# Joining the small products of three token mixers into fewer, larger steps between GEMM matmuls

## The chip, the cores and the metric

The kernel runs on one core of a Trainium2 chip. The metric is the device time of one execution in microseconds (us), the median over runs.

## The reference

One layer of a hybrid decoder: 512 tokens behind 16 learned meta tokens, width 1024, all in float32.

```python
h = RMSNorm(z);  P = h @ W_in
y = sigmoid(G_gla)*(GLA(P) W_a) + sigmoid(G_rwkv)*(RWKV7(P) W_b) + sigmoid(G_hgrn)*(HGRN2(P) W_c)
z = z + y @ W_out
z = z + ConvFFN(RMSNorm(z))        # D_FF 2816, then a last RMSNorm
...
# GLA (4 heads) and HGRN2 (4 heads), in chunks
scores = einsum('bhnid,bhnjd->bhnij', q * exp(b - b_ref), k * exp(b_ref - b))      # masked causal
o_intra = einsum('bhnij,bhnjv->bhniv', scores, v)
inc = einsum('bhnjd,bhnjv->bhndv', k * exp(b_last - b), v)
s_next = dec[..., None] * s + inc
o_inter = einsum('bhnid,bhndv->bhniv', q * exp(b), s_start)
...
# RWKV7 (8 heads of 64): S is 64x64 per head
s = s * w_t + sa[..., None] * (kk_t * a_t) + v_t[..., None] * k_t      # sa = -S kk_t
y_t = S r_t
```

## The kernel before, in words

**GEMMs.** The projections are computed transposed, 128 output columns at a time and all 528 (or 512) tokens in two halves. Each float32 weight tile is split on ACT (L202) and DVE (L203) into two float16 parts, and three float16 products are summed for each pair, so PE runs thousands of matmuls of 128x128 weights on 256 to 272 columns ("GEMM matmul" below; out `g`). Three weight buffers w0 to w2 rotate; the GEMM's outputs use two pairs of PSUM banks, g0 and g1.

**Mixers.** GLA, HGRN2 and RWKV7 need many small float32 products: transposes, scores of chunks, state updates, with meta tokens (16 rows) treated apart. Their outputs use a ring of four PSUM banks: each call of `bank` takes the next, and PE waits until the former user of that bank has been copied out by ACT or DVE. `lin_mixer` (L580 on) serves four HGRN2 heads (hg0 to hg3, one head each) and GLA (gl0, gl1, two heads each). Its steps: transposes of k (`pk`, `pmt`), of v (`pv`, one per head), state of the meta tokens and increments (`ps0`, `pin`), scores (`pc`), those of the meta tokens (`pcm`), outputs (`po`), meta outputs (`pom`), transposed outputs (`pt`, `ptm`). `rw_phase1` prepares pairs of RWKV7 heads i=0 to 3 (`psu`, `psa`, norms of k in `pss`, `prb`, `pM`, meta `pMm`). An inversion of triangular blocks runs on DVE (L1194, L1199). `rw_phase2` forms `pQ`, `pN`, transposes `tA`, `tB`, `tK`, `tV`, the meta part `tm` with `pmm`, then `psb`, `psx`, `p1`, `p2`, `pw`, `ph`/`py`, `pf`, and a chain of eight steps `pc` for two heads each, which hands a state on through a copy to HV (L1473, L1474), with a norm (L1440 to L1444) and `pyt` behind it.

**What sets the order.** On PE the order is the program's own. `drive` runs all mixers as generators: a mixer yields (delay, banks wanted) ahead of a step and is resumed when PE's modelled time has passed the delay, so many banks are modelled free, and enough GEMM matmuls have been issued since the last step (0.7 of that step's modelled time, and always one matmul at least). The delays stand in the table LT. What a mixer issues between two yields is called a step here; between two steps lie GEMM matmuls. The order on DVE, ACT and POOL is made by a scheduler from priorities, so it moves when the steps do.

```python
        yield LT["pk"][im], 2
...
            yield LT["pv"], 1
...
                    owed = LT["mix"] * (pe.t - t0) + 0.01
```

Of the kernel before, what the change touches and what calls it, by code (L numbers as in the profile page):

```python
# [48 lines left out]
LT = dict(  # L49
    f=17.0, pk=(1.0, 1.89, 0.0, 0.0, 1.0, 0.0), pv=0.0, ps0=1.2, pc=0.75,  # L50
    po=(4.08, 2.75, 0.98, 0.0, 0.0, 2.0), pt=(10.56, 10.58, 9.41, 18.52, 18.27, 9.18), gk=0.75, v=0.0,
    gv=4.09, k=4.31, pss=(1.14, 1.4, 0.28, 1.69), prb=(2.37, 3.25, 2.02, 2.9),
    pM=(2.7, 3.05, 4.48, 2.95), pMm=0.0, r=18.93, rv=0.9, g=1.82, T=53.8, pN=0.0, tA=2.44, tB=0.0, tK=0.8,
    tm=3.44, psb=1.1, psx=1.06, p1=11.9, p2=3.06, pw=5.19, ph=0.44, pf=0.1, ch0=0.0, ch=3.4, gn=3.11, y=9.68,
    hold=1.85, mix=0.7,
)
# [38 lines left out]
def trunk(ctx: ExitStack, tc: tile.TileContext, d: dict, out: bass.AP):  # L95
# [486 lines left out]
    def lin_mixer(im, gev, nm, gsum, gscale, q, k, vs, sgs, normw, ys):  # L582
# [84 lines left out]
        vec.tensor_copy(S[:, 0], ps0)  # L667
        for t in range(3):
            vec.scalar_tensor_tensor(S[:, t + 1], S[:, t], DT[:, t : t + 1], pin[:, t, :], ALU.mult, ALU.add)


        yield LT["pc"], 2
# [27 lines left out]
        for pcm, hr in zip(pcms, hrs):  # L700
            pe.matmul(pcm, lhsT=k1[hr, 0:16], rhs=q1[hr, 14:16], start=True, stop=True)
        for (st, stm), pcm in zip(stv, pcms):
            vec.copy_predicated(stm, maskC[0:16, 14:16], pcm)
# [526 lines left out]
    def rw_phase2(i, r1, E0, ANs, Xs, HVs, s2, s2m, s3):  # L1230
# [75 lines left out]
        pa = tok4(f"tA{i}", Ap, 0)
        for rr, kc in par:
            act.activation(AN[rr, :, :, rr], pa[rr], AF.Copy)

        for h, hr in enumerate(hrs):  # L1310
            for q, (rr, sr_) in enumerate(par):
# [9 lines left out]
        pk = tok4(f"tK{i}", Kd, 16)
        for q, (rr, sr_) in enumerate(par):
            act.activation(E[sr_, q:8:2, :, sr_], pk[sr_], AF.Copy)
        yield f"v{i}"
        yield 0.0, 1

# [486 lines left out]
```

## Time and profile before

| | |
|---|---|
| runs | 1023.19, 1027.21, 1027.33 us; median 1027.21 |
| profiled execution | 1026.22 us, span 1023.9, granted clock 0.99 |
| busy PE / weight loads (PEld) / DVE / ACT / POOL | 96 / 76 / 62 / 46 / 14% of the span |

The mixers run from about 30 to 580 us, the last GEMMs and the FFN behind them. Records of PE overlap, since a matmul drains while the next streams: distances between starts tell what one costs, not the length of a record. A float32 product is two records on PE. Waits are given as "engine waits for a tile <- engine and line that released it".

### The profile page before, as it was taken

What the parts mean: (1) busy time and instruction counts of PE and PEld (TensorE: products, weight loads), DVE (VectorE), ACT (ScalarE), POOL (GpSimd) and SP (SyncE); (2) the same over time, 40 slices, a digit from 0 to 9 for tenths busy, and PEclk for the clock granted to TensorE, in tenths of its full rate; (3) what the DMA queues carried; (4) which work ended last, traced back from release to release, by engine and by line L of the source; (5) the groups of instructions that cost most, each with busy time, mean ns of one, the idle gap of its engine ahead of it and who ended that gap; (6) DMA issues with size and microseconds to landing.
All of it is one profiled execution on the core that took longest, in us unless ns stands there. A gap on an engine that the chain in (4) does not pass through costs nothing.

```text
span 1023.9 us, 20898 instructions
## 1 busy us (share of the span) xinstructions
PE 984.7 (96%) x8694; PEld 775.6 (76%) x8694; DVE 638.2 (62%) x1234; ACT 467.1 (46%) x882; POOL 140.4 (14%) x307
## 2 busy tenths in 40 slices
PE   8999989999999989999999989999999999999996
PEld 7888877887778868788878874488888888854442
DVE  5677655445677998677644485567777677783211
ACT  6767565435654444344433353553334443552100
POOL 3122211201333511111000123000000000000100
PEclk9999999999999999999999999999999999999999
DMA  6322222233224314122233463023333333472100
GB/s 192 106 69 58 63 63 83 63 94 81 84 70 115 91 46 126 39 67 63 59 87 84 126 226 106 1 84 104 104 92 96 102 104 104 146 229 99 42 14 28
DMA packets 149289, 92.35 MB, mean 90 GB/s; under 512 B 17664, under 2 KB 142073, under 8 KB 149195
## 3 DMA queue, kind: packets, MB, share of 16 engines
q1 hardware_dynamic: 149195, 91.02, 31.3%
q8 instruction: 68, 1.11, 0.5%
q14 instruction: 26, 0.21, 0.1%
HBM read 86.92 MB, written 3.95 MB: 89 GB/s over the span
## 4 chain that ended last, share of the span: by engine, by line
PE 72%; DVE 12%; ACT 7%; DMA 3%; issue 3%; POOL 2%; SPq 0%; POOLq 0%; DVEq 0%; ACTq 0%
PE g L70 56%; PE dn L70 6%; DVE w L203 2%; DVE AN L1199 1%; DVE HV L1194 1%; DMA wf<-in_w_out_dram 1%; PE pc L70 1%; ACT w L202 1%; PE pf L70 1%; PE hT L75 1%; PE pw L70 1%; PE pogl L70 1%; ACT L383 1%; DMA z<-in_x_dram 1%; PE pcgl L70 0%
## 5 line engine op out<-in xcount | busy, mean ns | idle before, releaser
L70 PEld LDWEIGHTS <-w 128*128 128x128 f16 x5856 | 570.2, 99 | 89.4 <-issue 9.2
L70 PE MATMUL g<-hT,w 128*128 128x256 f16 (+3 forms) x5280 | 620.5, 274 | 2.6 <-ACT siluhg L383 2.2
L203 DVE SCALAR_TENSOR_TENSOR w<-wf,w 128x1024 f16<-128x1024 f32 (+1 forms) x131 | 150.7, 1151 | 93.8 <-ACT w L202 93.5
L202 ACT ACTIVATE w<-wf 128x1024 f16<-128x1024 f32 (+1 forms) x131 | 130.6, 999 | 108.0 <-PE g L70 96.1
L70 PEld LDWEIGHTS <-hid 128*128 128x128 f16 x528 | 51.7, 98 | 63.0 <-issue 1.1
L70 PE MATMUL g<-y,w 128*128 128x258 f16 x576 | 75.3, 273 | 3.5 <-DVE y L447 2.0
L1691 DVE SCALAR_TENSOR_TENSOR c<-u,parB,c 128x512 f32<-128x512 f32 x88 | 66.1, 751 | 2.4
L70 PE MATMUL g<-wd,hid 128*128 128x512 f16 x264 | 57.3, 379 | 0.8 <-DVE z L1742 0.8
L70 PE MATMUL dn<-wd,hid 128*128 128x512 f16 x264 | 57.1, 379 | 0.0
L1746 POOL TENSOR_SCALAR ssf<-ssf 128x1 f32<-128x1 f32 x4 | 2.2, 540 | 311.2 <-ACT sq L1744 311.1
L70 PE MATMUL g<-woh,mT 128*128 128x512 f16 x128 | 38.9, 379 | 0.6 <-DVE z L1645 0.6
L1709 ACT ACTIVATE c<-c 128x512 f32<-128x512 f32 x22 | 13.9, 630 | 53.8 <-DVE c L1691 53.8
L1744 ACT ACTIVATE sq<-z 128x512 f32<-128x512 f32 x8 | 5.0, 628 | 72.3 <-DVE z L1742 72.3
L70 PEld LDWEIGHTS <-mT 128*128 128x128 f16 x192 | 18.5, 98 | 24.2 <-issue 2.9
L1725 DVE SCALAR_TENSOR_TENSOR wd<-wf,wd 128x1024 f16<-128x1024 f32 x22 | 26.9, 1224 | 15.6 <-ACT wd L1724 15.4
L1724 ACT ACTIVATE wd<-wf 128x1024 f16<-128x1024 f32 x22 | 23.3, 1057 | 25.1 <-DMA wf<-in_w_down_dram 25.1
L1443 POOL TENSOR_TENSOR gv<-gv,mhalf 128x2 f32<-128x2 f32 (+1 forms) x16 | 13.9, 876 | 136.2 <-DVE gv L1442 136.2
L1742 DVE SCALAR_TENSOR_TENSOR z<-g,z 128x512 f32<-128x512 f32 x4 | 2.8, 692 | 45.8 <-PE g L70 45.8
L383 ACT ACTIVATE u<-g 128x258 f32<-128x258 f32 x88 | 29.2, 373 | 0.0
L1474 ACT ACTIVATE HV<-pc 64x128 f32<-64x128 f32 x32 | 8.4, 272 | 42.8 <-DVE HV L1473 39.4
L70 PE MATMUL g<-wol,mT 128*128 128x512 f16 x64 | 24.3, 379 | 0.0
L1689 DVE TENSOR_SCALAR c<-u,parB 128x512 f32<-128x512 f32 x44 | 23.8, 542 | 0.0
(484 smaller groups left out, 1195.6 us busy)
## 6 DMA issues: line engine op xcount, KB each, us to landing
wf<-in_w_in_dram SPq DMA_DIRECT2D x65, 512.0 KB
wf<-in_w_up_dram SPq DMA_DIRECT2D x44, 512.0 KB
wf<-in_w_down_dram SPq DMA_DIRECT2D x22, 512.0 KB
wf<-in_w_out_dram SPq DMA_DIRECT2D x8, 512.0 KB
xt<-in_x_dram SPq DMA_DIRECT2D x4, 512.0 KB
wf<-in_w_out_hg_dram SPq DMA_DIRECT2D x8, 256.0 KB
wf<-in_w_out_gla_dram SPq DMA_DIRECT2D x8, 256.0 KB
...
```

Source lines behind the costliest of these rows:

```text
L70: r = self.eng.matmul(out, lhsT=lhsT, rhs=rhs, **kw)
L75: r = self.eng.transpose(out, in_, ident)
L202: act.activation(wh[:, :kt, :m], wf[:, :kt, :m], AF.Copy, scale=WS)
L203: vec.scalar_tensor_tensor(wl[:, :kt, :m], wf[:, :kt, :m], WS, wh[:, :kt, :m], ALU.mult, ALU.subtract)
L383: act.activation(dst[:m, off + c0 : off + c0 + n], src, func, **kw)
L1194: eng.tensor_tensor(u, bc(mats[:, j, j + 1 : n], c1 - c0), Ti[:, j, c0:c1].unsqueeze(1).broadcast_to([cnt, r, c1 - c0]), op=ALU.mult)
L1443: gps.tensor_tensor(var, var, mhalf[:, 0 : 2 * n].rearrange("p (a b) -> p a b", b=2), op=ALU.pow)
L1689: vec.tensor_scalar(c, u[:, 0:SEQ], colB(52 + j), colB(8 + j), ALU.mult, ALU.add)
L1691: vec.scalar_tensor_tensor(c, u[:, t : t + SEQ], colB(52 + 44 * t + j), c, ALU.mult, ALU.add)
L1709: act.activation(cg, cg, AF.Silu)
L1724: act.activation(wd[f][:, 0], wf, AF.Copy, scale=WS)
L1725: vec.scalar_tensor_tensor(wd[f][:, 1], wf, WS, wd[f][:, 0], ALU.mult, ALU.subtract)
```

## The change

Two steps become one where the second had only been put behind a yield; what belongs together also shares banks:

- `lin_mixer`: `pv` of all heads follows `pk` in one step, which asks for 2 banks and one more per head. `pcm` moves from behind `pc` into the step of `ps0`/`pin` and uses free columns of their banks. `pom` moves from behind `po` to behind `pc`, in one bank for all heads, and is copied out after `po`.
- `rw_phase1`: the five products `pss` lose the yields between them. `pMm` joins `pM` in its banks.
- `rw_phase2`: `pmm` moves from the `tm` step to `pN`, in its banks; its six copies to Xm, Em, Nm come before those of `pN`. `tA` and `tB` become one step, `tK`, `tV` and `tm` another (3 banks). `ph`/`py` join `pw` in one bank. The two heads of a chain step follow each other with no yield.
- The delays in LT become one number per mixer, with the same values. Lines shift by 29 to 31.

```diff
-        yield LT["pk"][im], 2
+        yield LT["pk"][im], 2 + nh
...
         for h in range(nh):
-            yield LT["pv"], 1
             pv = bank(f"pv{nm}{h}", P, 4, P)
...
-        yield LT["ps0"], 2
-        ps0 = bank(f"ps0{nm}", P, P)
-        pin = bank(f"pin{nm}", P, 3, P)
+        yield LT["ps0"][im], 2
+        psb0, pinb = bank(f"ps0{nm}", P, 512), bank(f"pin{nm}", P, 512)
+        ps0, pin = psb0[:, 0:P], pinb[:, 0 : 3 * P].rearrange("p (t n) -> p t n", n=P)
+
+        pcms = [psb0[0:16, P : P + 2], pinb[0:16, 3 * P : 3 * P + 2]][:nh]
...
+        for pcm, hr in zip(pcms, hrs):
+            pe.matmul(pcm, lhsT=k1[hr, 0:16], rhs=q1[hr, 14:16], start=True, stop=True)
+        for (st, stm), pcm in zip(stv, pcms):
+            vec.copy_predicated(stm, maskC[0:16, 14:16], pcm)
...
         for (st, stm), pc in zip(stv, pcs):
             vec.copy_predicated(st, maskC.unsqueeze(1).broadcast_to([P, 4, P]), pc)
-        yield 0.0, 2
-        pcms = [bank(f"pcm{nm}{h}", 16, 2) for h in range(nh)]
...
+        poms = bank(f"pom{nm}", 2, nh, P)
+        for h in range(nh):
+            pe.matmul(poms[:, h, :], lhsT=stv[h][1], rhs=mt[:, 1 + h, :], start=True, stop=True)
...
-        yield 0.0, 2
-        poms = [bank(f"pom{nm}{h}", 2, P) for h in range(nh)]
-        for h, pom in enumerate(poms):
-            pe.matmul(pom, lhsT=stv[h][1], rhs=mt[:, 1 + h, :], start=True, stop=True)
...
             pe.matmul(pss[:, t, :], lhsT=kq[:, 16 + P * t : 16 + P * (t + 1)], rhs=ind2, start=True, stop=True)
-            yield 0.0, 0
...
+        for pm, hr in zip(pms, hrs):
+            pe.matmul(pm, lhsT=BKm[hr, 0], rhs=AR[hr, 0, 0:16], start=True, stop=True)
...
-        yield LT["pMm"], 2
-        pms = [bank(f"pMm{i}{h}", 16, 16) for h in range(2)]
...
-        yield LT["tA"], 1
+        yield LT["tA"][i], 2
         pa = tok4(f"tA{i}", Ap, 0)
+        pb = tok4(f"tB{i}", Bd, 16)
...
-        yield LT["tB"], 1
-        pb = tok4(f"tB{i}", Bd, 16)
...
-        yield LT["tK"], 1
+        yield LT["tK"][i], 3
         pk = tok4(f"tK{i}", Kd, 16)
...
-        yield LT["tm"], 2
...
-        pms = [bank(f"pmm{i}{h}", 16, 20) for h in range(2)]
...
-        yield LT["pw"], 2
+        yield LT["pw"][i], 3
...
-        yield LT["ph"], 2
-        ph = bank(f"phm{i}", 64, 2, 64)
-        py = bank(f"pym{i}", 2, 2, 64)
+        phy = bank(f"phm{i}", P, 512)
...
                     pe.matmul(pc[:, l, :], lhsT=E[:, c, l, :], rhs=HV[:, c, l, :], start=True, stop=True)
-                    if l == 0:
-                        yield 0.0, 0
```

PE in HGRN2 head 3 (`hg3`), before: `pcm` and `po` each stand as a step between GEMM matmuls (`g`).

```order
L70 MATMUL g_70<-hT,w_76 128x258
L70 MATMUL pcmhg_1836<-e1hg_1701,d1hg_1702 16x2
L70 LDWEIGHTS w_76
L70 MATMUL g_70<-hT,w_76 128x256
L70 MATMUL pohg_1840<-vthg_1763,st_409 128x128 x4
L70 MATMUL pohg_1840<-Shg_1765,q5hg_1730 128x128 x4
```

The same after the change, the steps of `ps0` and of `pc` (13 GEMM matmuls stand between `pomhg` and `pohg`, left out here).

```order
L101 MATMUL ps0hg_1786<-mthg_1748 128x128
L101 MATMUL pinhg_1787<-vthg_1755,kthg_1743 128x128 x3
L101 MATMUL ps0hg_1786<-e1hg_1698,d1hg_1699 16x2
...
L101 MATMUL pchg_1805<-qmhg_1731,kmhg_1732 64x64 x4
L101 MATMUL pchg_1805<-bhg_1696,dlhg_1706 32x32 x8
L101 MATMUL pomhg_1823<-mthg_1748,stm_410 2x128
```

`pcm` (16x2, out in the bank of `ps0`) and `pom` have moved ahead, behind other small products.

ACT in the first GLA pair (`gl0`), before: `vt` are copies of `pv`, `silu` and `w` belong to the GEMM.

```order
L653 ACTIVATE vtgl00_2169<-pvgl00_2164 128x512
L383 ACT_TABLE_LOAD
L383 ACTIVATE silugl00_2173<-g1_70 128x258
L383 ACTIVATE silugl00_2173<-g1_70 128x256
L202 ACTIVATE w0_74<-wf0_71 128x1024
L653 ACTIVATE vtgl01_2185<-pvgl01_2180 128x512
L594 ACT_TABLE_LOAD
L594 ACTIVATE e1gl1_2621<-d1gl1_2622 128x528
```

After:

```order
L683 ACTIVATE vtgl00_2152<-pvgl00_2147 128x512
L683 ACTIVATE vtgl01_2159<-pvgl01_2154 128x512
L625 ACT_TABLE_LOAD
L625 ACTIVATE e1gl1_2614<-d1gl1_2615 128x528
L634 ACTIVATE bgl1_2612<-bgl1_2612 128x512
L633 ACTIVATE dlgl1_2622<-dlgl1_2622 128x528
L626 ACTIVATE d1gl1_2615<-d1gl1_2615 128x528
L414 ACT_TABLE_LOAD
L414 ACTIVATE silugl00_2195<-g1_70 128x258
L414 ACTIVATE silugl00_2195<-g1_70 128x256
L233 ACTIVATE w0_74<-wf0_71 128x1024
```

The second `vt` has moved ahead of silu and the split of w0, and those behind the exponentials of gl1. On DVE, in the same place after the change, the other half of that split stands ahead of the copies to `st` (read by `po`); before, it stood ahead of `Sgl0`:

```order
L709 SCALAR_TENSOR_TENSOR Sgl0_2161<-Sgl0_2161,DTgl0_2103,pingl0_2174 128x128 x2
L234 SCALAR_TENSOR_TENSOR w0_74<-wf0_71,w0_74 128x1024
L733 COPY_PREDICATED st1_413<-maskC_95,pcgl00_2208 128x512
L733 COPY_PREDICATED st2_417<-maskC_95,pcgl01_2209 128x512
```

The split of w0 now comes later than all of `Sgl0` and right before both `st`.

PE at the start of RWKV7's first phase, before: the last transposes of GLA and then `psu`, `psa` of i=0.

```order
L75 MATMUL ptgl11_3024<-ident_77,ogl11_2884 128x128 x4
L75 MATMUL ptmgl11_3029<-ident_77,ogl11_2884 128x2
L70 LDWEIGHTS w2u0_2910
L70 MATMUL psu00_3079<-swu0_430,w2u0_2910 128x272
L70 LDWEIGHTS w2u0_2910
```

After, the transposes are followed by GEMM matmuls, 43 of them before `psu`:

```order
L106 MATMUL ptgl11_2967<-ident_77,ogl11_2823 128x128 x4
L106 MATMUL ptmgl11_2972<-ident_77,ogl11_2823 128x2
L101 LDWEIGHTS w0_74
L101 MATMUL g0_69<-hT_110,w0_74 128x258
```

## Rows read from the trace of the kernel before

**Rows 1.** Page: busy us, share, instructions by engine; below, the chain's shares

```profile
PE 984.7 (96%) x8694; PEld 775.6 (76%) x8694; DVE 638.2 (62%) x1234; ACT 467.1 (46%) x882; POOL 140.4 (14%) x307
...
PE 72%; DVE 12%; ACT 7%; DMA 3%; issue 3%; POOL 2%; SPq 0%; POOLq 0%; DVEq 0%; ACTq 0%
```

**Rows 2.** Windows: busy us of PE, PEld, DVE, ACT, POOL; granted clock; DMA

```profile
350.00:375.00 25.00, 22.28 (x227) 18.54 (x226) 24.53 (x62) 11.29 (x28) 4.69 (x5) 0.93 0.31 86
...
400.00:425.00 25.00, 25.00 (x358) 20.49 (x353) 18.65 (x48) 6.64 (x16) 1.83 (x3) 1.00 0.28 69
```

**Rows 3.** Waits of PE, 30 to 600 us: us in total, times, longest

```profile
PE tA L75 <- issue: 2.7, 1, 2.7
PE pingl L70 <- ACT vtgl L653: 2.5, 1, 2.5
PE g L70 <- ACT siluhg L383: 2.2, 1, 2.2
PE pyt L75 <- DVE HV L1444: 2.2, 1, 2.2
PE psb L70 <- DVE Nm L1351: 1.8, 1, 1.8
...
PE psa L70 <- DVE ygl L741: 1.0, 1, 1.0
...
PE prb L75 <- DVE Mt L1108: 0.9, 1, 0.9
PE pw L70 <- ACT AN L1308: 0.8, 1, 0.8
...
PE pc L70 <- ACT HV L1474: 0.4, 1, 0.4
```

**Rows 4.** Timeline of PE: start, length, line, operation, count

```profile
47.47 0.60 PE L75 MATMUL pvhg<-ident,v 128*128 128x128 f32 x4
47.91 0.38 PE L70 MATMUL g<-hT,w 128*128 128x256 f16 x2
...
142.05 1.37 PE L70 MATMUL g<-hT,w 128*128 128x258 f16 x11
143.35 0.20 PE L70 MATMUL pcmhg<-e1hg,d1hg 128*16 128x2 f32 x2
143.48 0.28 PE L70 MATMUL g<-hT,w 128*128 128x256 f16 x1
```

**Rows 5.** Window behind siluhg (columns of rows 2), then timeline of PE

```profile
132.90:136.40 3.50, 3.50 (x19) 2.76 (x18) 1.55 (x2) 1.93 (x5) 0.00 (x0) 0.51 0.53 135
...
133.33 1.28 PE L70 MATMUL g<-hT,w 128*128 128x258 f16 x5
134.40 1.06 PE L75 MATMUL pvhg<-ident,v 128*128 128x128 f32 x4
```

**Rows 6.** Timeline of PE at a chain step

```profile
461.12 0.33 PE L70 MATMUL pc<-HV,E 128*128 128x64 f32 x2
461.29 0.27 PE L70 MATMUL g<-hT,w 128*128 128x256 f16 x1
461.40 0.33 PE L70 MATMUL pc<-HV,E 128*128 128x64 f32 x2
```

**Rows 7.** Timeline of DVE before pyt

```profile
520.00 1.22 DVE L203 SCALAR_TENSOR_TENSOR w<-wf,w 128x1024 f16<-128x1024 f32 x1
521.14 0.28 DVE L1441 TENSOR_REDUCE gv<-ARBK 128x2 f32<-128x128 f32 x1
```

**Rows 8.** Timeline of ACT in gl0, then of DVE

```profile
174.59 1.28 ACT L383 ACT_TABLE_LOAD   x1
...
177.37 0.60 ACT L653 ACTIVATE vtgl<-pvgl 128x512 f32<-128x512 f32 x1
...
185.32 1.34 DVE L697 COPY_PREDICATED st<-maskC,pcgl 128x512 f32<-128x512 int32 x2 [3.64 <-PE pcgl L70]
```

**Rows 9.** Timeline of DVE in phase 2 of i=0

```profile
367.94 1.75 DVE L1304 TENSOR_TENSOR AN<-pN,maskL 64x256 f32<-64x256 f32 x4
```

More of the change, by code (lines that the diff above doesn't have):

```diff
@@ L49 @@
 LT = dict(
[L50 to L55, printed above, removed]
+    f=17.0,
+    pk=(1.0, 1.89, 0.0, 0.0, 1.0, 0.0),
+    pv=(0.0, 0.0, 0.0, 0.0, 0.0, 0.0),
+    ps0=(1.2, 1.2, 1.2, 1.2, 1.2, 1.2),
+    pc=(0.75, 0.75, 0.75, 0.75, 0.75, 0.75),
+    po=(4.08, 2.75, 0.98, 0.0, 0.0, 2.0),
+    pt=(10.56, 10.58, 9.41, 18.52, 18.27, 9.18),
+    gk=0.75,
+    v=0.0,
+    gv=4.09,
+    k=4.31,
+    pss=(1.14, 1.4, 0.28, 1.69),
+    prb=(2.37, 3.25, 2.02, 2.9),
+    pM=(2.7, 3.05, 4.48, 2.95),
+    pMm=(0.0, 0.0, 0.0, 0.0),
+    r=18.93,
+    rv=0.9,
+    g=1.82,
+    T=53.8,
+    pN=(0.0, 0.0, 0.0, 0.0),
+    tA=(2.44, 2.44, 2.44, 2.44),
+    tB=(0.0, 0.0, 0.0, 0.0),
+    tK=(0.8, 0.8, 0.8, 0.8),
+    tm=(3.44, 3.44, 3.44, 3.44),
+    psb=(1.1, 1.1, 1.1, 1.1),
+    psx=(1.06, 1.06, 1.06, 1.06),
+    p1=(11.9, 11.9, 11.9, 11.9),
+    p2=(3.06, 3.06, 3.06, 3.06),
+    pw=(5.19, 5.19, 5.19, 5.19),
+    ph=(0.44, 0.44, 0.44, 0.44),
+    pf=(0.1, 0.1, 0.1, 0.1),
+    ch0=(0.0, 0.0, 0.0, 0.0),
+    ch=(3.4, 3.4, 3.4, 3.4),
+    gn=(3.11, 3.11, 3.11, 3.11),
+    y=9.68,
+    hold=1.85,
+    mix=0.7,
 )
@@ L666, in lin_mixer @@
                 pe.matmul(pin[hr, t, :], lhsT=kt[:, t, hr], rhs=vt[h][:, t, :], start=True, stop=True)
[L667 to L672, printed above, removed]
         stv = []
@@ L676, in lin_mixer @@
             nst[0] += 1
+        for pcm, hr in zip(pcms, hrs):
+            pe.matmul(pcm, lhsT=k1[hr, 0:16], rhs=q1[hr, 14:16], start=True, stop=True)
+        for (st, stm), pcm in zip(stv, pcms):
+            vec.copy_predicated(stm, maskC[0:16, 14:16], pcm)
+        vec.tensor_copy(S[:, 0], ps0)
+        for t in range(3):
+            vec.scalar_tensor_tensor(S[:, t + 1], S[:, t], DT[:, t : t + 1], pin[:, t, :], ALU.mult, ALU.add)
+        yield LT["pc"][im], nh + 1
         pcs = [bank(f"pc{nm}{h}", P, 4, P) for h in range(nh)]
@@ L697, in lin_mixer @@
             vec.copy_predicated(st, maskC.unsqueeze(1).broadcast_to([P, 4, P]), pc)
-        yield 0.0, 2
-        pcms = [bank(f"pcm{nm}{h}", 16, 2) for h in range(nh)]
[L700 to L703, printed above, removed]
+        poms = bank(f"pom{nm}", 2, nh, P)
+        for h in range(nh):
+            pe.matmul(poms[:, h, :], lhsT=stv[h][1], rhs=mt[:, 1 + h, :], start=True, stop=True)
         outs = []
-        yield LT["po"][im], 2
+        yield LT["po"][im], nh
         pos = [bank(f"po{nm}{h}", P, 4, P) for h in range(nh)]
@@ L713, in lin_mixer @@
                 pe.matmul(po[:, t, :], lhsT=q5[hr, P * t : P * (t + 1)], rhs=S[hr, t, :], start=False, stop=t == 3)
-        yield 0.0, 2
-        poms = [bank(f"pom{nm}{h}", 2, P) for h in range(nh)]
-        for h, pom in enumerate(poms):
-            pe.matmul(pom, lhsT=stv[h][1], rhs=mt[:, 1 + h, :], start=True, stop=True)
-        for h, (po, pom) in enumerate(zip(pos, poms)):
+        for h, po in enumerate(pos):
             o = lt.tile([P, 5, P], F32, tag="o", name=f"o{nm}{h}")
@@ L721, in lin_mixer @@
             act.activation(o[:, 0:4], po, AF.Copy)
-            vec.tensor_copy(o[0:2, 4], pom)
+            vec.tensor_copy(o[0:2, 4], poms[:, h, :])
             oq = lt.tile([P, 5, P], F32, tag="oq", name=f"oq{nm}{h}", bufs=1)
@@ L1098, in rw_phase1 @@
         yield LT["pM"][i], 2
-        pqs = [bank(f"pM{i}{h}", P, 4, 64) for h in range(2)]
+        pMs = [bank(f"pM{i}{h}", P, 512) for h in range(2)]
+        pqs = [b[:, 0:256].rearrange("p (t n) -> p t n", n=64) for b in pMs]
+        pms = [b[0:16, 256:272] for b in pMs]
         for c in range(8):
@@ L1106, in rw_phase1 @@
                 )
-        for h, pq in enumerate(pqs):
+        for pm, hr in zip(pms, hrs):
+            pe.matmul(pm, lhsT=BKm[hr, 0], rhs=AR[hr, 0, 0:16], start=True, stop=True)
+        for h, (pq, pm) in enumerate(zip(pqs, pms)):
             vec.tensor_copy(Mt[:, :, h, :], pq)
-        yield LT["pMm"], 2
-        pms = [bank(f"pMm{i}{h}", 16, 16) for h in range(2)]
-        for h, (pm, hr) in enumerate(zip(pms, hrs)):
-            pe.matmul(pm, lhsT=BKm[hr, 0], rhs=AR[hr, 0, 0:16], start=True, stop=True)
             vec.tensor_copy(Mtm[:, h, :], pm)
@@ L1292, in rw_phase2 @@
                 vec.tensor_tensor(E[sr_, q:8:2, h, rr], pq[sr_, 4 * q : 4 * q + 4, :], mU[sr_], op=ALU.mult)
-        yield LT["pN"], 2
-        pns = [bank(f"pN{i}{h}", P, 4, 64) for h in range(2)]
+        yield LT["pN"][i], 2
+        pNs = [bank(f"pN{i}{h}", P, 512) for h in range(2)]
+        pns = [b[:, 0:256].rearrange("p (t n) -> p t n", n=64) for b in pNs]
+        pms = [b[0:16, 256:276] for b in pNs]
         for c in range(8):
@@ L1301, in rw_phase2 @@
                 )
-        for h, (pn, hr) in enumerate(zip(pns, hrs)):
-            for q, (rr, sr_) in enumerate(par):
-                vec.tensor_tensor(AN[rr, :, h, sr_], pn[rr], mL[rr], op=ALU.mult)
-        yield LT["tA"], 1
[L1306 to L1311, printed above, removed]
-                vec.tensor_tensor(E[rr, q:8:2, h, rr], main64(AR[hr, 1, 16:T])[:, q:8:2, :], bc(g0[hr, q:8:2], 64), op=ALU.mult)
-                gps.tensor_tensor(
-                    E[rr, q:8:2, h, sr_], ident[hr, hr].unsqueeze(1).broadcast_to([64, 4, 64]), bc(Dc[hr, q:8:2], 64), op=ALU.mult
-                )
-        yield LT["tB"], 1
-        pb = tok4(f"tB{i}", Bd, 16)
-        for rr, kc in par:
-            act.activation(X[rr, :, :, kc], pb[rr], AF.Copy)
-        yield LT["tK"], 1
[L1321 to L1325, printed above, removed]
-        pv = bank(f"tV{i}", P, 4, P)
-        for t in range(4):
-            pe.matmul(pv[:, t, :], lhsT=sv[:, 16 + P * t : 16 + P * (t + 1)], rhs=cen, start=True, stop=True)
-        pv = pv.rearrange("p t (h n) -> p t h n", n=64)
-        for q, (rr, sr_) in enumerate(par):
-            act.activation(HV[sr_, q:8:2, :, :], pv[sr_], AF.Copy)
-        yield LT["tm"], 2
-        pm = bank(f"tm{i}", 16, 3, P)
-        for j, src in enumerate((Bd, Kd)):
-            pe.transpose(pm[:, j, :], src[:, 0:16], ident)
-        pe.matmul(pm[:, 2, :], lhsT=sv[:, 0:16], rhs=cen, start=True, stop=True)
-        pm4 = pm.rearrange("p a (h n) -> p a h n", n=64)
-        act.activation(Xm[:, :, 2:66], pm4[:, 0], AF.Copy)
-        act.activation(Em[:, :, 2:66], pm4[:, 1], AF.Copy)
-        act.activation(Vm, pm4[:, 2], AF.Copy)
-        pms = [bank(f"pmm{i}{h}", 16, 20) for h in range(2)]
         for pm, hr in zip(pms, hrs):
@@ L1351, in rw_phase2 @@
             vec.tensor_tensor(Nm[:, h, :], pm[:, 4:20], maskL[0:16, 0:16], op=ALU.mult)
-        yield LT["psb"], 2
+        for h, (pn, hr) in enumerate(zip(pns, hrs)):
+            for q, (rr, sr_) in enumerate(par):
+                vec.tensor_tensor(AN[rr, :, h, sr_], pn[rr], mL[rr], op=ALU.mult)
+        yield LT["tA"][i], 2
+        pa = tok4(f"tA{i}", Ap, 0)
+        pb = tok4(f"tB{i}", Bd, 16)
+        for rr, kc in par:
+            act.activation(AN[rr, :, :, rr], pa[rr], AF.Copy)
+        for h, hr in enumerate(hrs):
+            for q, (rr, sr_) in enumerate(par):
+                vec.tensor_tensor(E[rr, q:8:2, h, rr], main64(AR[hr, 1, 16:T])[:, q:8:2, :], bc(g0[hr, q:8:2], 64), op=ALU.mult)
+                gps.tensor_tensor(
+                    E[rr, q:8:2, h, sr_], ident[hr, hr].unsqueeze(1).broadcast_to([64, 4, 64]), bc(Dc[hr, q:8:2], 64), op=ALU.mult
+                )
+        for rr, kc in par:
+            act.activation(X[rr, :, :, kc], pb[rr], AF.Copy)
+        yield f"v{i}"
+        yield LT["tK"][i], 3
+        pk = tok4(f"tK{i}", Kd, 16)
+        for q, (rr, sr_) in enumerate(par):
+            act.activation(E[sr_, q:8:2, :, sr_], pk[sr_], AF.Copy)
+        pv = bank(f"tV{i}", P, 4, P)
+        for t in range(4):
+            pe.matmul(pv[:, t, :], lhsT=sv[:, 16 + P * t : 16 + P * (t + 1)], rhs=cen, start=True, stop=True)
+        pv = pv.rearrange("p t (h n) -> p t h n", n=64)
+        for q, (rr, sr_) in enumerate(par):
+            act.activation(HV[sr_, q:8:2, :, :], pv[sr_], AF.Copy)
+        pm = bank(f"tm{i}", 16, 3, P)
+        for j, src in enumerate((Bd, Kd)):
+            pe.transpose(pm[:, j, :], src[:, 0:16], ident)
+        pe.matmul(pm[:, 2, :], lhsT=sv[:, 0:16], rhs=cen, start=True, stop=True)
+        pm4 = pm.rearrange("p a (h n) -> p a h n", n=64)
+        act.activation(Xm[:, :, 2:66], pm4[:, 0], AF.Copy)
+        act.activation(Em[:, :, 2:66], pm4[:, 1], AF.Copy)
+        act.activation(Vm, pm4[:, 2], AF.Copy)
+        yield LT["psb"][i], 2
         rw_bonus(i)
         yield "g"
-        yield LT["psx"], 2
+        yield LT["psx"][i], 2
         lg = sv[:, 0:NY]
@@ L1407, in rw_phase2 @@
             act.activation(X[:, 2 * t2 : 2 * t2 + 2].rearrange("p t h n -> p (t h) n"), pw, AF.Copy)
-        yield LT["ph"], 2
-        ph = bank(f"phm{i}", 64, 2, 64)
-        py = bank(f"pym{i}", 2, 2, 64)
+        phy = bank(f"phm{i}", P, 512)
+        ph, py = (phy[:n, o : o + 128].rearrange("p (a b) -> p a b", b=64) for n, o in ((64, 0), (2, 128)))
         for l in range(2):
@@ L1427, in rw_phase2 @@
         yield "out27"
-        yield LT["ch0"], 1
+        yield LT["ch0"][i], 1
         Y = HV[:, 0:9:2]
@@ L1462, in rw_phase2 @@
         nb = 2 if i >= CH2 else 1
-        pcs = [bank(f"pc{i}{l}", P, 8 // (3 - nb), 64, hold=8 * (LT["ch"] + 0.5)) for l in range(nb)]
+        pcs = [bank(f"pc{i}{l}", P, 8 // (3 - nb), 64, hold=8 * (LT["ch"][i] + 0.5)) for l in range(nb)]
         for c in range(8):
```

10 lines of the change are left out of this document (5 added, 5 removed).

## Prediction, made before the changed kernel was timed

> **What bounds the kernel now.** Start with the share of busy time: PE is busy 984.7 of 1023.9 us, and the chain of work that ended last is 72% PE [rows 1]. So the time is PE's own work, plus the gaps in which PE has nothing that it may start, plus the stretches in which its clock is low. The windows tell where these lie [rows 2]: from 350 to 375 us PE is idle for 2.7 us at a DVE that is busy for 24.5 of 25, while from 400 to 425, with mixers beside it too, it has no idle time. The sums are made against the profiled execution, 1026.22 us (span 1023.9 and 2.3 around it); it stands 1.0 below the median of 1027.21.
>
> The waits of PE between 30 and 600 us, where the mixers run, are few and each has its name [rows 3]. What PE waits for after 600 us belongs to the tail, which the change doesn't touch.
>
> Two more kinds of loss show. The first are **edges**, where PE turns from a GEMM matmul to a small product and back; starts in the timeline give their price [rows 4]. Eleven GEMM matmuls from 142.05 take 0.11 each (1.37 for all, less a last record of 0.27, is 1.10 for ten) and should end at 143.25. The two passes of pcm start at 143.35, and the GEMM goes on at 143.48: 0.23 us for two columns of work, 0.10 on the way in and the rest on the way out. Four full 128x128 transposes (pv) take 0.44 from their start to the next GEMM matmul, 0.11 each, with no edge to see.
>
> The second are **clock dips**: 132.9 to 136.4, just behind the wait for siluhg, runs at a granted clock of 0.51, the lower of the two levels (1.2 of 2.4 GHz), and five GEMM matmuls from 133.33 to 134.40 take 0.21 each [rows 5].
>
> **The change, part by part.** No arithmetic is added. PE's order shows 232 turns from GEMM to small products before and 147 after. What a removed turn saves depends on whether the shape of the weights still changes inside the joined step.
>
> *Chain heads.* 32 pairs of heads lose the GEMM matmul between them. One head starts at 461.12, GEMM at 461.29, the next head at 461.40 [rows 6]: 0.17 per head. Its two passes have half the columns of a transpose of 0.11, so 0.055 each; 0.06 is the way out. The join saves one of two: 32 x 0.06 = 1.9. Bounds: 0 if the second head's weights keep the array as long as the turn did, 3.7 if the whole 0.115 behind a first pass goes.
>
> *pss.* Four ways out in each of four mixers: 16 x 0.06 = 1.0 (0 to 1.8). *pMm* behind pM, which uses the same 64 rows: one or two edges of 0.10, 0.15 x 4 = 0.6 (0.4 to 0.8). *pom* behind pc's narrow products likewise: 0.15 x 6 = 0.9 (0 to 1.2). *pcm* behind pin: pin's weights are full for HGRN2 as the GEMM's are, so both edges stay: 0 (to 1.4, six times 0.23). *pmm* goes from tm to pN and loses one change of shape: 4 x 0.10 = 0.4 (0 to 0.8). ph/py behind pw and the joins of pv, tA with tB and tK with tV have full-shape neighbours: 0.3 together. **Sum of the edges: 5.1, between 1 and 9.**
>
> A rule speaks against this term. By the Trainium skill (TensorE: Matmul & The Clock Gate, "Step-by-step: what each phase is for") the PE pulls a weight load ahead of matmuls in flight when the load targets the background weight buffer. By that rule the turns would be free already, the term 0 and the time rival B's. The trace agrees for pv and differs for pcm, with its 0.10 in and 0.10 out.
>
> *Waits that go* [rows 3]. psa (1.0) waits for the bank of ptgl, copied late by DVE; in the new order 43 GEMM matmuls lie between instead of none: -1.0. prb (0.9) waits for the copy of Mt out of a bank; pMm takes no bank any more, so the ring shifts: -0.9. pw (0.8): its bank's copy is 22 GEMM matmuls old: -0.8. pyt (2.2): on DVE the reduction at 521.14 that starts the norm chain stood behind a w split of 1.22 [rows 7]; in the new order it comes first, so at least 1.1 of the wait goes and at most 2.2; I take 1.6, since other copies leave the chain too. g for siluhg (2.2): on ACT y came behind v3 and a split and held up silu's table load; now y comes ahead of v3, and a split for gk is queued earlier; between 0 and 2.2, I take -1.2. Sum -5.5.
>
> *Waits that come.* In gl0 pin waited 2.5 for vtgl01, which stood behind a table load (1.28), silu and a split on ACT until 177.37 [rows 8]. Now vtgl01 follows vtgl00 directly, but pk and both pv are one step, so ps0 and pin come about 0.9 sooner, and I leave pin 1.0 of its wait. Next, silu and the split move behind e1's four exponentials and two table loads, and DVE's half of that split stands ahead of the two st copies (1.34 together, at 185.32 [rows 8]) that po needs: the split of 1.22 [rows 7] and most of a table load are newly in po's way, 2.0 (0 to 3.8, a load, a split and the copies). Net 1.0 + 2.0 - 2.5 = +0.5. In phase 2 of i=0, tB follows tA at once and needs pQ's second bank, which DVE empties with pieces of 0.44 (the four AN pieces of 64x256 take 1.75 [rows 9]): +0.6. The AN pieces start behind six little Xm, Em and Nm pieces, and tK's step waits for their bank: +1.5, between 0 and 2.7 (tA's wait). psb's 1.8 for Nm goes. Net +0.3. The same in i=1, milder: +0.3. In chain 2 HV's copy on DVE now stands behind pQ3's eight pieces, two gates and a split: pc's wait of 0.4 [rows 3] becomes 1.5 (0.4 to 3.9, eight pieces): +1.1. gl1's po: +0.2. Sum +2.4. Who waits for these is PE alone, and behind it the GEMM's own two banks, whose copies on ACT and DVE have time then. A new order also has waits that I do not see; four of the size of pc's 0.4 make 1.5, which I add.
>
> *Clock.* 3.4 us at half clock lose 1.7 us. If siluhg's wait halves, the dip behind it may vanish: half of that, -0.9.
>
> **Sum:** -5.1 - 5.5 + 2.4 + 1.5 - 0.9 = -7.6, and 1026.2 - 7.6 = **1018.6**.
>
> **The rivals.**
> *A. Banks eat the gains.* Joined steps ask for more of the four banks at once: pk for 3 (4 in GLA), tK's for 3, pw for 3. A step that waits for the last of three copies waits longer than the first of three steps did. For it: half the rows of group 3 are waits for copies out of a bank (psa, prb, pw, tA). Against it: 400 to 425 us has no idle PE [rows 2]. Price: six pk and four tK steps at 0.5 each, between pc's 0.4 and pw's 0.8: +5.0, 1023.6.
> *B. Edges do not shrink*, because the changes of shape remain inside the joined steps, or because a turn was free to begin with. For it: pcm behind pin, and pv's 0.11 each. Against it: 0.17 per head where the passes fill 0.11. Price: 1018.6 + 5.1 = 1023.7. (The Trainium skill's rule above would give this case.)
> *C. Slower: the DVE-bound inversion stalls every joined transpose step.* PE stands in order, so tA+tB and tK+tV+tm hold all GEMM behind them until DVE has emptied the banks. tA of i=0 already waits 2.7 with DVE at 24.5 of 25. If the joined steps wait as long in all four phases 2 and each wait drops the clock as in rows 5, each costs 2.7 + 1.7 = 4.4; the first is in the sum: 3 x 4.4 = +13.2, 1031.8. It decides from the point at which three waits reach 2.5 us. Against it: DVE falls to 18.65 from 400 us on.
> That the change does not reach the program as meant is no rival: PE's order shows the joined steps.
>
> **How the numbers follow.** A change of 0.5%, 5.1 us, is about what a measurement of this kernel can tell from none; from the median, faster is below 1022.1 and slower above 1032.3. Chances: forecast 0.53 (its own range is 1013 to 1023), A 0.20, B 0.10, C 0.17. A and B lie near 1023.6, within 0.5%, and a quarter of each reaches under 1022; a tenth of the forecast lies over it: faster 0.48 + 0.07 = 0.55. C spreads from 1028 to 1036, most of it over 1032.3: slower 0.14. Same is what is left, 0.31. With the edges at 9 and the new waits at half the sum gives 1010 or so; C's middle is near 1031.8. From 1010 to 1031 the range leaves out half of C and the lowest of the forecast, about 2 in 10 with what no case here covers.
>
> **What would show it.** Right: no GEMM matmul between the heads of a chain step, and 0.28 from the first head to the GEMM; psa, prb and pw gone from PE's waits; pyt under 1.0; new waits of po for st in gl0 and of pc in chain 2; PE idle for 2 to 4 us less. Wrong: tA, tB or tK at the head of PE's waits with over 2 us in i=1 to 3; another stretch at half clock; edges inside the joined steps as long as before.

## The result, and the profile after

The changed kernel takes 1013.25 us (median of 4 runs, 1012.57 to 1013.55), beside 1025.2 before (4 runs, 1022.29 to 1027.33) on the same chip: ratio 0.9898, interval 0.9879 to 0.9916. By the ratio that is faster by 10.5 us. The two medians lie 12.0 apart, and from the 1023.0 that the kernel before took in the later comparisons it is 9.8. The forecast was 1018.6, with a range from 1010 to 1031.

First the page of the changed kernel, the lines that answer to [rows 1]:

```profile
span 1011.4 us, 20895 instructions
...
PE 981.4 (97%) x8694; PEld 777.5 (77%) x8694; DVE 636.0 (63%) x1234; ACT 466.7 (46%) x881; POOL 136.8 (14%) x307
...
PE 78%; DVE 12%; ACT 5%; DMA 3%; issue 2%; POOL 1%; SPq 0%; POOLq 0%; DVEq 0%; ACTq 0%
```

The span falls by 12.5 us from 1023.9. PE's busy time falls by only 3.3 (984.7 to 981.4); its idle time, span less busy, falls by 9.2, from 39.2 to 30.0. So in these two executions three quarters of the gain are idle time of PE. The number of instructions on PE is unchanged.

Busy time is longer where the clock is low, so the windows come next; columns as in [rows 2]. Two of the kernel before:

```profile
125.00:150.00 25.00, 21.34 (x205) 17.60 (x203) 12.70 (x23) 17.31 (x28) 3.41 (x16) 0.93 0.25 66
175.00:200.00 25.00, 22.48 (x232) 18.29 (x229) 12.52 (x25) 13.53 (x21) 3.35 (x10) 0.86 0.16 43
```

and of the changed kernel:

```profile
125.00:150.00 25.00, 23.28 (x237) 19.71 (x236) 16.10 (x30) 18.93 (x33) 5.62 (x20) 1.00 0.24 65
...
175.00:200.00 25.00, 23.07 (x210) 20.06 (x208) 14.10 (x22) 8.84 (x18) 4.78 (x4) 1.00 0.32 77
...
350.00:375.00 25.00, 20.95 (x173) 16.92 (x171) 24.21 (x76) 11.24 (x28) 3.71 (x5) 0.93 0.22 57
375.00:400.00 25.00, 21.74 (x264) 17.66 (x263) 16.58 (x45) 11.04 (x21) 2.44 (x4) 0.93 0.42 104
```

The granted clock gives what was lost: 25 us at 0.93 lose 1.75, at 0.86 3.5. Before, 125 to 150, 175 to 200 and 350 to 375 [rows 2] lost 7.0 together; after, only 350 to 400 loses, 3.5. (The first 25 us stand at 0.93 in both, and the last few are low in both.) That difference, 3.5, is all of the 3.3 by which PE's busy time fell. **Nothing is left for the edges.**

The clock's part holds for these two executions alone. Over the runs on record the granted clock has the same mean, 0.9925, for the changed kernel (4 runs) and for the kernel before (the 43 runs of the later comparisons). So on the average the clock gave nothing, and the gain that stays, 9.8, is about the idle time, 9.2.

The waits of PE between 30 and 620 us in the changed kernel, in total, times, longest:

```profile
PE tA L106 <- DVE ARBK L1320: 3.0, 1, 3.0
PE tA L106 <- issue: 2.4, 1, 2.4
PE pogl L101 <- DVE st L733: 1.8, 1, 1.8
...
PE pohg L101 <- DVE st L733: 1.3, 1, 1.3
PE pc L101 <- ACT HV L1497: 1.2, 1, 1.2
PE tB L106 <- DVE E L1320: 1.0, 1, 1.0
...
PE g L101 <- ACT siluhg L414: 0.4, 1, 0.4
...
PE tK L106 <- DVE AN L1343: 0.4, 1, 0.4
PE tV L101 <- DVE AN L1343: 0.3, 1, 0.3
```

Against [rows 3]: pin's 2.5, pyt's 2.2, psb's 1.8, psa's 1.0, prb's 0.9 and pw's 0.8 are gone, and siluhg is down from 2.2 to 0.4. New or longer are po for st in gl0 (1.8), pc in chain 2 (1.2, was 0.4), tB (1.0), tK and tV (0.7 together, tK had 0.3) and, largest of all, tA of i=1 for 3.0 (was 0.4). Also gone, and not in the forecast, is a wait of 2.0 of the GEMM for y at 603 us, this row of the kernel before:

```profile
PE g L70 <- DVE y L447: 2.2, 2, 2.0
```

ACT in gl0 of the changed kernel shows the mechanism of the wait that pin had [rows 8]; the two copies vtgl follow each other, and the split of w is behind:

```profile
167.46 1.07 ACT L683 ACTIVATE vtgl<-pvgl 128x512 f32<-128x512 f32 x2
...
173.44 1.28 ACT L414 ACT_TABLE_LOAD   x1
174.73 0.66 ACT L414 ACTIVATE silugl<-g 128x258 f32<-128x258 f32 x2
175.28 1.06 ACT L233 ACTIVATE w<-wf 128x1024 f16<-128x1024 f32 x1
```

And DVE before tA of i=1: half the rows of pQ cannot be moved into X until a DMA has read X's former content (the inversion's result, on its way to DRAM), and tA wants the first of pQ's two banks. The second of these lines waits 5.12 for that DMA; in the kernel before, the last line, the same wait was 1.87.

```profile
375.33 0.43 DVE L1320 TENSOR_TENSOR ARBK<-pQ,maskU 64x256 f32<-64x256 f32 x1
380.88 0.43 DVE L1319 TENSOR_TENSOR X<-pQ,maskU 64x256 f32<-64x256 f32 x1 [5.12 <-DMA s<-X]
...
390.51 0.43 DVE L1291 TENSOR_TENSOR X<-pQ,maskU 64x256 f32<-64x256 f32 x1 [1.87 <-DMA s<-X]
```

**What the joined steps cost** is read from starts on PE in the timeline. A joined pair of heads and a joined pss:

```profile
435.29 0.56 PE L101 MATMUL pc<-HV,ARBK 128*128 128x64 f32 x4
435.68 0.38 PE L101 MATMUL g<-hT,w 128*128 128x256 f16 x2
...
254.58 1.08 PE L101 MATMUL pss<-ind,kq 128*128 128x2 f32 x10
255.59 0.40 PE L101 MATMUL g<-y,w 128*128 128x258 f16 x2
```

The pair lasts 0.39 from its first start to the GEMM, against 2 x 0.17 for two single heads [rows 6]: 0.05 **more**, not 0.06 less. pss lasts 1.01. Of the kernel before, two of the five singles at i=1:

```profile
284.77 0.28 PE L70 MATMUL pss<-ind,kq 128*128 128x2 f32 x2
284.91 0.27 PE L70 MATMUL g<-hT,w 128*128 128x256 f16 x1
...
285.66 0.28 PE L70 MATMUL g<-hT,w 128*128 128x272 f16 x1
285.86 0.20 PE L70 MATMUL pss<-ind,kq 128*16 128x2 f32 x2
```

Each takes 0.14 until the GEMM goes on, and the way into the last, narrow one another 0.09 (285.66 to 285.86, less a GEMM matmul): 0.79 for the five.

The starts inside tell where this comes from. Behind a GEMM matmul the first pass of a head is followed by its second after 0.055. In a joined pair only this first distance is short; each later pass is followed 0.11 after its start, the second head's first pass too: 0.055 + 3 x 0.11 = 0.39. So it is with the full passes of pss, whose first distance is 0.03. The weight-load records of the pair's four passes also start 0.11 apart. A GEMM matmul's own columns take 0.11, so there such a start costs nothing; a product of 2 or 64 columns does not cover it. That the weight loads are the reason is argued from these starts; no run tried it.

The kernel before has a row that comes near to this and that the prediction did not use:

```profile
356.00 2.00 PE L70 MATMUL pQ<-ARBK 64*128 64x64 f32 x32
```

These are 32 passes of 64 columns on weights of 64 rows and 128 columns. They start in 16 pairs (one pass on each half of the rows, 0.007 apart), and the pairs start about 0.11 apart, not 0.055.

### The profile page after: what moved, and what is told of

The parts are those of the page before. It is cut to its first block, busy times and chain, and to the rows that moved or that the text cites. A ratio compares the mean times of both kernels' runs of the same rounds, so it can differ in the third digit from the quotient of the medians.

```text
span 1011.4 us, 20895 instructions
## 1 busy us (share of the span) xinstructions
PE 981.4 (97%) x8694; PEld 777.5 (77%) x8694; DVE 636.0 (63%) x1234; ACT 466.7 (46%) x881; POOL 136.8 (14%) x307
## 4 chain that ended last, share of the span: by engine, by line
PE 78%; DVE 12%; ACT 5%; DMA 3%; issue 2%; POOL 1%; SPq 0%; POOLq 0%; DVEq 0%; ACTq 0%
PE g L101 60%; PE dn L101 6%; DVE w L234 2%; PE pc L101 1%; DVE HV L1222 1%; DVE AN L1227 1%; PE pf L101 1%; DVE wol L1606 1%; ACT w L233 1%; PE pw L101 1%; DMA s<-X 1%; ACT L414 1%; PE hT L106 1%; PE pogl L101 1%; PE pohg L101 1%
## 5 line engine op out<-in xcount | busy, mean ns | idle before, releaser
L101 PE MATMUL g<-hT,w 128*128 128x256 f16 (+3 forms) x5280 | 610.1, 274 | 1.3 <-DVE acc L478 0.6
L101 PE MATMUL g<-y,w 128*128 128x258 f16 x576 | 71.1, 273 | 1.4 <-DVE gate L478 1.3
L101 PEld LDWEIGHTS <-mT 128*128 128x128 f16 x192 | 18.5, 98 | 24.2 <-issue 2.9
```

The source lines that it names most:

```text
L101: r = self.eng.matmul(out, lhsT=lhsT, rhs=rhs, **kw)
```

## The experiments

Two theories were set against each other: **W**, the gain is waits and clock dips, moved by new orders on ACT and DVE; and **E**, the prediction's edges (what a turn from GEMM to a small product and back costs). All ratios are against runs of the kernel before on the same chip.

**e1, e2: heads apart again, then pss too** (edits of the changed kernel).

```diff
                     pe.matmul(pc[:, l, :], lhsT=E[:, c, l, :], rhs=HV[:, c, l, :], start=True, stop=True)
+                    if l == 0:
+                        yield 0.0, 0
...
             pe.matmul(pss[:, t, :], lhsT=kq[:, 16 + P * t : 16 + P * (t + 1)], rhs=ind2, start=True, stop=True)
+            yield 0.0, 0
```

> The changed kernel with only the two heads of a chain step apart again (one GEMM matmul between them). Theory W (waits): the change gained by waits and clock dips, its joins save PE nothing; a joined pair of heads lasts 0.393 us from its first start to the GEMM, two single heads 2 x 0.169 = 0.338, so taking 32 of them apart makes the time 1.8 us shorter, about 1011.5 from 1013.25, if the waits stay. Theory E (edges, the prediction's): a pair apart costs 0.06 more, so the time is 1.9 longer, about 1015.1. Where waits move, the sum of starts within chain steps still tells: -1.8 by W, +1.9 by E.

> As e1, and the five products pss are apart again too. Theory W: a joined pss lasts 1.015 us, its five singles with their ways in and out 0.79, so four mixers save 0.9 more: 1010.6. Theory E: apart costs 1.0 more: 1016.1. The orders of DVE and ACT move a good deal here, so waits may move by 1 to 2 us either way.

Measured: e1 1012.55 us, 0.9897 (0.9882 to 0.9911); e2 1010.15, 0.9873 (0.9848 to 0.9898); the changed kernel 0.9898. E's +1.9 and +2.9 don't come. W's -1.8 does not show in e1, which equals the changed kernel within the interval; its -2.7 fits e2, which is faster by 0.25%, at the edge of what can be told. A step of e1's chain has its records back at 0.33 for two, with the GEMM between (434.36 to 434.63 is 0.17 and one GEMM matmul):

```profile
434.36 0.33 PE L101 MATMUL pc<-HV,ARBK 128*128 128x64 f32 x2
434.63 0.33 PE L101 MATMUL pc<-HV,ARBK 128*128 128x64 f32 x2
```

Waits moved as well: tA of i=1 fell to 1.3 in e1, and pyt came back with 0.7 there and 2.7 in e2. So joining heads and pss brings nothing, and the price of the join shows in the records.

**e3, e4, e7, e10: one part of the change alone**, in the kernel before: the joins of HGRN2 and GLA; of RWKV7's first phase; of its second without the heads; the heads. Each is a part of the diff ahead of the prediction; the yields that go tell which (lines between them are left out, and `...` parts the four groups):

```diff
...
-            yield LT["pv"], 1
-        yield 0.0, 2
-        pcms = [bank(f"pcm{nm}{h}", 16, 2) for h in range(nh)]
-        yield 0.0, 2
-        poms = [bank(f"pom{nm}{h}", 2, P) for h in range(nh)]
...
-            yield 0.0, 0
-        yield LT["pMm"], 2
...
-        yield LT["tB"], 1
-        yield 0.0, 1
-        yield LT["tm"], 2
-        yield LT["ph"], 2
...
-                    if l == 0:
-                        yield 0.0, 0
```

The four groups are e3, e4, e7 and e10 in this order.

> The kernel before with only the joins of the HGRN2 and GLA mixers (pv to pk, pcm to ps0, pom to pc). Theory W: what these mixers wait for goes: siluhg 2.4 to 0.6, pin's 2.7 in gl0 gone and po's 2.0 there instead, psa's 1.2 gone, and the clock dips at 133 (1.7) and 177 (3.3) gone: 7 to 9 us, about 1017. Theory E: edges of these joins, 0.9 for pom and 0.2 for pv: about 1024. Both say a little less if waits of RWKV7 move.

> The kernel before with only the joins of RWKV7's first phase (pss without yields, pMm in the step of pM). Theory W: pss joined costs 4 x 0.22 = 0.9 more, pMm saves 4 x 0.1 = 0.4; prb's wait for a bank (1.1) goes; together -0.6, about 1024.6. Theory E: -1.0 for pss, -0.6 for pMm and the wait: -2.7, about 1022.5.

> The kernel before with the joins of RWKV7's second phase alone, without the chain heads (pmm to pN, tA with tB, tK with tV and tm, ph and py to pw). Theory W: psb's 2.0 and pw's 1.0 go; tA with tB adds 1.1 and 0.4 in i=0, tK and tV 0.5 more; the dip at 365 stays: -1 to -2. Theory E: 0.4 + 0.3 from edges and the same waits. Rival C of the prediction (joined transposes stall): +3 or more.

> The kernel before with only the chain heads joined. By the records of the changed kernel a joined pair takes 0.393 instead of 2 x 0.169, 32 x 0.055 = +1.8; the prediction said -1.9. Waits ahead of gl0 to 400 us cannot move by it, those after (psx 0.5, pc 0.55, pyt 2.4, g for y 2.2) can: theory W +1.8 if they stay, 0 to -3 if pyt's goes; theory E -1.9 and the same.

Measured: e3 1015.07, ratio 0.992 (0.9905 to 0.9934); e4 1023.02, 0.9998 (0.9982 to 1.0013); e7 1018.39, 0.9949 (0.9933 to 0.9964); e10 1021.94, 0.9995 (0.9982 to 1.0007). e3 is as W said, 8 us, with E's 1024 excluded. e4 agrees with W's small gain and not with E's 2.7. In e10 neither sign shows: pyt's wait fell from 2.2 to 1.7, psb's from 1.8 to 1.0 and y's at 603 us left the waits over 1.0, while pc's rose to 1.2; that would cover the 1.8 (32 x 0.055) that the heads cost. e7 brought 4.7, more than either theory gave it and against rival C; psb, pw and y are not among PE's waits over 1.0 there, and pin's 2.5 still is.

**e5, e6: which join of HGRN2 and GLA.** e5 has pv behind pk alone, e6 pcm and pom alone: the first line of e3's group, and the other four.

```diff
-            yield LT["pv"], 1
...
-        pcms = [bank(f"pcm{nm}{h}", 16, 2) for h in range(nh)]
...
-        poms = [bank(f"pom{nm}{h}", 2, P) for h in range(nh)]
```

> The kernel before with one join alone: the transposes pv follow pk in one step. No edge is saved (full weights on both sides), so theory E gives no change, within 0.5 us. Theory W: vtgl01 comes out of its place behind silu and the split on ACT, so pin's wait of 2.7 in gl0 goes and with it the clock dip behind it (3.3 us); a wait of po there of up to 2.0 may come. Between -4 and -6 us, ratio near 0.995.

> The kernel before with pcm in the step of ps0 and pom in that of pc alone, pv apart. Theory E: -0.9 for pom's edges. Theory W: the edges give -0.6; pin's wait for vtgl01 in gl0 stays with its dip; what the removed banks of pcm and pom bring is open (psa's 1.2 waits for a bank): -1 to -3. If most of the 8 us of the joins of these mixers is here, theory W has the wrong join.

Measured: e5 1017.97, 0.9948 (0.993 to 0.9966), as W said. e6 1013.61, 0.9897 (0.9862 to 0.9932): **the whole gain of the change**, from joins that W gave 1 to 3 us. W's own condition for being wrong is met: it had the wrong join, or rather no single one. In e6 pv is a step of its own, and still vtgl01 follows vtgl00 on ACT:

```profile
168.43 1.07 ACT L684 ACTIVATE vtgl<-pvgl 128x512 f32<-128x512 f32 x2
169.52 1.28 ACT L414 ACT_TABLE_LOAD   x1
170.81 0.66 ACT L414 ACTIVATE silugl<-g 128x258 f32<-128x258 f32 x2
```

pin has no wait in e6, po for st has none, and 175 to 200 us has full clock and no idle PE:

```profile
175.00:200.00 25.00, 25.00 (x230) 21.98 (x229) 14.20 (x26) 11.03 (x19) 5.46 (x12) 1.00 0.34 84
```

Either join moves ACT's order past the same bad place. The waits of siluhg (all but 0.2 to 0.4), psa and pw are gone in e3, e5 and e6 alike, and pin's too (0.4 is left in e5), 6 us or so each time. So the parts don't add up: 8.0 and 5.1 and 9.4 are largely the same microseconds. What gives e6 more than e3, which has its joins and pv's, was not tried.

**e9: that place by itself.** One yield of the kernel before is left out, between the two pv of gl0.

```diff
-            yield LT["pv"], 1
+            if (im, h) != (4, 1):
+                yield LT["pv"], 1
```

> The kernel before with one single yield removed: the second head's pv of gl0 follows the first with no GEMM between. PE's order changes only around there, ACT's in 8 rows, DVE's in 11; vtgl01 now follows vtgl00 on ACT, ahead of silu and the split. Theory W: pin's wait of 2.7 in gl0 goes, and the two dips' worth of half clock behind it (3.3 us): -5 to -6 of 1023, ratio 0.994 to 0.995, with nothing from edges (one full-shape join). Rival: gl0's wait is made up for by a later one (po for st 2.0, as in the changed kernel), then -2 to -4. Rival E: no change.

Measured: 1019.67, 0.9964 (0.995 to 0.9978): faster by 3.4, less than W's 5 to 6. Between 175 and 200 us ACT's order and the clock did what W said:

```profile
174.34 1.06 ACT L654 ACTIVATE vtgl<-pvgl 128x512 f32<-128x512 f32 x2
175.42 1.28 ACT L383 ACT_TABLE_LOAD   x1
...
175.00:200.00 25.00, 25.00 (x278) 21.09 (x275) 15.14 (x30) 15.35 (x24) 5.91 (x11) 1.00 0.20 51
```

and no wait of po for st took its place. But behind pyt, whose wait of 2.2 was there before too, half clock followed this time, and 4 us at 0.64 lose 1.4. Over the runs the granted clock is no higher than before (0.993 in the mean of e9's 5 runs and of the 14 beside them), so the 3.3 that W counted for the dips did not come, and 3.4 is little more than pin's wait of 2.5.

```profile
518.00:522.00 4.00, 4.00 (x25) 3.00 (x24) 0.77 (x2) 0.77 (x3) 0.00 (x0) 0.64 0.47 128
```

**e8, e11: fill the waits instead.** e8 is e2 with later steps; e11 also has ph/py apart and longer delays.

```diff
-    pk=(1.0, 1.89, 0.0, 0.0, 1.0, 0.0),
+    pk=(2.6, 1.89, 0.0, 0.0, 1.0, 0.0),
-    po=(4.08, 2.75, 0.98, 0.0, 0.0, 2.0),
+    po=(4.08, 2.75, 0.98, 3.1, 4.1, 2.0),
-    tA=(2.44, 2.44, 2.44, 2.44),
+    tA=(6.3, 3.6, 2.44, 2.44),
-    tK=(0.8, 0.8, 0.8, 0.8),
+    tK=(2.4, 1.4, 0.8, 0.8),
-    psb=(1.1, 1.1, 1.1, 1.1),
+    psb=(4.3, 1.1, 1.1, 1.1),
```

(e11, other lines of the table left out; e8 had po 1.5 and 2.1, tA 5.1 and 3.6, tK and psb as before.)

> The kernel of e2 with four waits of PE taken up by later steps in the table of delays: pk of hg0 +1.6 us, po of hg3 +1.5, po of gl0 +2.1, tA of i=0 +2.7 and of i=1 +1.2, so that GEMM matmuls fill what PE waited (1.5, 1.45, 2.3, 2.6 and 1.2, 9.0 in all) and the dip behind tA (1.7) does not come. If PE's waits are what the time is made of (theory W), 6 to 10 us less than e2, 1001 to 1004. If what is filled here comes back as waits later on, because the inversion on DVE or the copies on ACT set the pace, no change from e2's 1010.

> As e8, with ph and py apart from pw again and the delays that had no effect there made longer, since GEMM time owed for the step before already covered them: po of hg3 3.1 and of gl0 4.1, tA of i=0 6.3, tK 2.4 and 1.4 in i=0 and 1, psb of i=0 4.3. If waits are what is left (theory W), another 3 to 6 us less than e8's 1008: 1002 to 1005; if DVE's inversion sets the pace there, the waits come back behind it and it stays at 1007 to 1009.

Measured: e8 1007.92, 0.9848 (0.9818 to 0.9877); e11 1006.45, 0.9836 (0.9822 to 0.985). Both missed what W gave them (1001 to 1004, 1002 to 1005), though e11 is the fastest of all, 0.6% under the changed kernel; it is nearer to what its rival said (1007 to 1009). In e8 the two delays of po changed nothing (po still waits 1.8 and 1.2), probably since the GEMM time owed for the step before was already longer; tA's wait went, and psb's came back behind it with 2.8. In e11 po's waits are gone, and those of the inversion stretch return at other steps:

```profile
PE pN L101 <- DVE ARBK L1321: 3.1, 2, 1.9
PE psx L101 <- issue: 2.1, 1, 2.1
...
350.00:375.00 25.00, 19.41 (x173) 15.74 (x170) 24.23 (x74) 11.04 (x25) 0.95 (x1) 1.00 0.30 82
```

With DVE at 24.2 of 25 us from 350 to 375 (24.2 to 24.5 in the two kernels compared here), a wait that is filled there moves on. Where ACT's order was at fault, in gl0, reordering pays (e9); what filling po's waits in e11 is worth was not tried apart from the rest.

## Why the prediction was right or wrong

**The total** lay in the range, and its sign was right, but in part by luck: the sum of -7.6 against the measured -10.5 (-13.1 between the two profiled executions, 1026.22 and 1013.14, the first of which the sum starts from) hides two large errors of opposite sign. What the prediction named as signs of being wrong all came: tA at the head of PE's waits with 3.0 in i=1, a new stretch with low clock (375 to 400), and edges inside the joined steps no shorter than before. The 0.28 from the first head to the GEMM that would have shown it right is 0.39, and PE's idle time fell by 9.2 where 2 to 4 was named.

**The edges, -5.1, are the step that failed.** "The join saves one of two" took 0.055 for each pass of a head and the remaining 0.06 for a way out to the GEMM that a join would save. But 0.055 is only the distance behind the first pass after a GEMM matmul; every other pass is followed after 0.11, by the GEMM or by the next small product, as e1's and the changed kernel's records show. By starts: heads 32 x 0.055 = +1.8 instead of -1.9; pss 4 x 0.22 = +0.9 instead of -1.0. The narrow joins came nearer. pom and pMm apart, in the kernel before:

```profile
147.66 0.83 PE L70 MATMUL g<-hT,w 128*128 128x256 f16 x6
148.41 0.38 PE L70 MATMUL pomhg<-mthg,stm 16*2 16x128 f32 x2
148.72 0.51 PE L70 MATMUL g<-hT,w 128*128 128x256 f16 x3
...
295.76 0.94 PE L70 MATMUL g<-y,w 128*128 128x256 f16 x7
296.63 0.22 PE L70 MATMUL pMm<-ARBK,BKm 64*16 64x16 f32 x4
296.78 0.28 PE L70 MATMUL g<-y,w 128*128 128x258 f16 x1
```

and joined, in the changed one:

```profile
52.63 0.38 PE L101 MATMUL pomhg<-mthg,stm 16*2 16x128 f32 x2
52.94 0.50 PE L101 MATMUL g<-hT,w 128*128 128x258 f16 x3
...
283.67 0.22 PE L101 MATMUL pM<-ARBK,BKm 64*16 64x16 f32 x4
283.82 0.40 PE L101 MATMUL g<-y,w 128*128 128x258 f16 x2
```

Apart, pom takes 0.40 from when it was due (six GEMM matmuls of 0.11 from 147.66) to the GEMM's start, joined 0.31; pMm 0.25 and 0.15. That saves 0.1 each, -0.6 for six pom (said -0.9) and -0.4 for four pMm (said -0.6). By their starts the joins of pcm in HGRN2 (said 0), of pmm (said -0.4) and of ph/py save nothing. Together the edges come to about +1.7. PE's busy time, less what the clock lost, rose by only 0.2, so something of about -1.5 stands against them that was not found. The Trainium skill's rule that was weighed there (TensorE: Matmul & The Clock Gate, "Step-by-step: what each phase is for"), that a weight load is pulled ahead of matmuls in flight, would have given 0, nearer than the row's reading. The trace differs from it at a narrow pcm, which still shows its 0.10 in and 0.10 out. What made the term wrong was the price of a small product behind another small one. The bounds (0 saved at the least) left no room for a loss, although pQ's row of the kernel before has 0.11 for a pass of 64 columns where the prediction took 0.055.

**Waits that go, -5.5.** Each of the five named waits went: psa, prb and pw whole, as said; pyt whole (2.2, said 1.6), siluhg by 1.8 (said 1.2). Right as to which go, and too small in size by 1.2. prb's goes with pMm's join alone (e4); the other causes were not tried one by one.

**Waits that come, +2.4 and 1.5.** po for st in gl0 was 1.8 (said 2.0), pc in chain 2 1.2 (said 1.5), tB of i=0 1.0 (said 0.6): right. pin's wait was put at 1.0 and is gone, and tK and tV wait 0.7, not 1.5. For i=1 +0.3 was said and tA waits 3.0, behind the DMA that reads X; the prediction had taken DVE alone for the bound there, though the 1.87 at this DMA stood in the trace. Not foreseen were y's 2.0 at 603 us, gone (the prediction had put what is behind 600 us out of the change's reach), and the wait of pss (1.0), gone. The 1.5 allowed for waits not seen had the wrong sign: more went than came.

**Clock, -0.9.** Three stretches with low clock became two, -3.5 in the profiled executions, and nothing in the mean of the runs (0.9925 for both kernels). The dip at 177 was left in the sum and went with pin's wait, as in e9; but in e10 pin still waits 2.5 and no dip follows. Nor is the one at 133 a sure consequence: in e9, e4, e7 and e10 siluhg still waits for 1.5 to 1.7 and no dip follows. So this belongs to the execution that was profiled (1026.22, against medians of 1023.0 of the kernel before in later comparisons); that fewer waits save clock is not shown.

**Rivals.** A (banks) did not happen: no joined pk is among the waits over 1.2 but that of hg0, which waits for k6 on DVE and not for a bank. B (no gain from edges) was right on its premise and wrong on its time, because waits gave more. C's size happened at one of four steps, with its dip, but behind a DMA and not DVE's own work, and was paid for elsewhere.

Why y at 603 us came in time was not tried; nor which of e7's joins brought its 4.7.
